# First column tiles of z instead of u, z stored from ScalarE's queue, gated-unit stream buffers lower, squares of x added on VectorE

## Chip, cores and metric

One NeuronCore of a Trainium2 chip runs the whole kernel. The metric is device time in microseconds; the kernel before takes 1092.7 us (median of 3 runs, 1092.6 to 1092.8).

## What is computed

A two-layer decoder trunk over 1024 positions of width 1024, in float32. The change touches layer 0:

```python
xn = rmsnorm(h, g)
u, z = jnp.split(xn @ in_w, [1024], axis=-1)
y = gelu(s5_ssm(u, ...) + d_skip * u)       # diagonal state space model over positions
y = y * sigmoid(y @ glu_w + glu_b)          # gated unit
y = y * silu(z)
h = h + y @ out_w
```

Then follow a shared K/V projection, a layer of differential attention, an out-projection and a last norm. Each float32 product of a matrix is made of three TensorE matmuls of `fp32r` parts.

## The kernel before, in words

Activations lie transposed: 8 row tiles of 128 channels by 1024 positions. `mm3` (L157 to L161) makes one product: high part by high part (L159), low part of the activation (L160), low part of the weight (L161). A column tile of a dense layer is 8 k-steps by 2 halves of 512 positions by these 3 matmuls, 48 in all (`mm_tile`, `dense`). A weight tile is loaded into `mraw` (one buffer), cast to `mhi` on ScalarE (ACT, L749) and its rest `mlo` is made on VectorE (DVE, L750); `mhi` and `mlo` have two buffers each. Accumulators of the dense layers are `ps` (4 banks, so two column tiles) and for the state space model `ps2` and `pb`.

Layer 0 begins while x is still arriving. For each of 8 row tiles of x, ACT casts `xh` and squares the tile (`rt`), DVE makes the rest `xl`, and TensorE (PE) does that k-step for three column tiles of u at once, with weights `fh` and `fl` (`first_u`). The sum of the squares over channels is taken on PE too: 32-column matmuls against ones (L526), in four column tiles of the array. From it come `rcol`, the broadcast row `R` (L688, L537), and the evacuation of u multiplied by `R` (L491). z needs no `R` here: it is evacuated as it is (L494) and multiplied by `R1` (the same row) in the gated unit (L623).

The state space model follows, for 8 channel tiles b, in units `t` (input powers and transposes, L310, L332), `c` (output powers `ca` and Toeplitz blocks, L362, L374 to L384), `u` (a column tile of u, stored to `ud`), `a` (apply: L392 on PE, then a chain of DVE operations from L401 to the last, L415, which writes the states `v`) and `o` (output: L424 on PE against `ca` and `toep`, GELU on ACT, L437, one half of the tile after the other, and a store to `yd` from ACT's queue, L439). `ORDER` lists the units. After them come the tiles 8 to 15 of the in-projection, which are z, and then the gated unit: `load_y` reads each `yd` back into `yr` (L595, issued by SyncE, SP), ACT casts `yh` (L610), DVE makes `yl` (L611), and 8 column tiles against `glu_w` follow. Per tile the gated unit's `done` loads z and y (`z`, `ya`), multiplies both on GpSimd (POOL, L623, L624), takes two sigmoids on ACT (L625 of z, L628 of the accumulator) and multiplies on DVE.

`ORDER` and the written sequence are only the start: the program is built with a scheduler that orders each engine's instructions by a timeline of its own, and every engine then runs its list strictly in order. Buffers with one name are used in turn: `yr` shares the names `ya`, `sg` and `z` (two buffers each) with the gated unit's own tiles.

Of the kernel before, what the change touches and what calls it, by code (L numbers as in the profile page):

```python
# [8 lines left out]
F32 = mybir.dt.float32  # L9
# [9 lines left out]
P = 128  # L19
SEQ = 1024  # L20
D = 1024
KT = D // P
# [11 lines left out]
NEG = -1e30  # L34


ORDER = ("t0 c0 t1 u3 a0 c1 o0 t2 u4 a1 c2 o1 t3 u5 a2 c3 o2 t4 u6 a3 c4 o3 t5 u7 a4 c5 o4 t6 a5 c6 o5 t7 a6 c7 o6 a7 "
         "o7").split()


# [14 lines left out]
class Trunk:  # L55
# [389 lines left out]
    def layer0(self, dbg=None):  # L445
        tc, nc, I = self.tc, self.nc, self.I
# [12 lines left out]
        with ExitStack() as es:  # L459
            sp, ev = pool(es, "ssm", 1), pool(es, "ev", 2)  # L460
            stp = ExitStack()
            tp = pool(stp, "stp", 1)
            R = self.R1
            pcr = self.ps3.tile([P, 2, 512], F32, name="pb")
            sqs = []

            pick = tp.tile([P, 2], F32, name="pick")
            G.memset(pick, 0.0)
            for r in range(4):
                G.memset(pick[32 * r:32 * r + 1, r // 2:r // 2 + 1], 1.0)  # L470

            ga = tp.tile([P, KT], F32, name="ga")
            nc.sync.dma_start(ga, I["ga"])

            def prep_x(k, cuts):
                raw = tp.tile([P, SEQ], F32, name="xraw", bufs=3)
                g = ga[:, k:k + 1]
                for c in cuts:
                    nc.sync.dma_start(raw[:, c], I["xT"][k * P:(k + 1) * P, c])
                    S.activation(xh[k][:, c], raw[:, c], AF.Copy, scale=g)  # L480
                    V.scalar_tensor_tensor(xl[k][:, c], raw[:, c], g, rd(xh[k][:, c]), op0=ALU.mult,
                                           op1=ALU.subtract)
                sqs.append(tp.tile([P, SEQ], F32, name="rt0", bufs=3))
                S.activation(sqs[k], raw, AF.Square)

            def evac(m, pt):
                for h in range(2):
                    hs = slice(h * 512, h * 512 + 512)
                    o = ev.tile([P, 512], F32, name="evo")
                    if m < KT:  # L490
                        V.tensor_mul(o, pt[h], R[:, hs])  # L491
                        nc.sync.dma_start(udv[m][:, hs], o)
                    else:
                        S.copy(o, pt[h])  # L494
                        nc.sync.dma_start(zds[m - KT][:, hs], o)


            pt0 = [[(ps if m < 2 else self.ps2).tile([P, 512], F32, name="ps") for h in range(2)] for m in range(3)]
            fst = ExitStack()
            fp = pool(fst, "first", 1)  # L500
            fw = []
            for k in range(KT):
                raw = fp.tile([P, 3 * P], F32, name="fw", bufs=3)
                hi = fp.tile([P, 3 * P], F32R, name=f"fh{k}")
                lo = fp.tile([P, 3 * P], F32R, name=f"fl{k}")
                nc.sync.dma_start(raw, I["in_w"][k * P:(k + 1) * P, 0:3 * P])
                S.copy(hi, raw)
                V.tensor_sub(lo, raw, rd(hi))
                prep_x(k, (slice(0, 512), slice(512, SEQ)) if k == 0 else (slice(0, SEQ),))
                if k == 0:  # L510
                    self.load_consts()
                    for i, pl in enumerate((tp, sp)):
                        self.load_small(i, pl.tile([P, CUTS[i + 1] - CUTS[i]], F32, name=f"small{i}"))
                fw.append((hi, lo))
            def first_u(k):
                for m in range(3):
                    ms = slice(m * P, (m + 1) * P)
                    self.mm_tile((fw[k][0][:, ms], fw[k][1][:, ms]), pt0[m], xh, xl, k)

            late = KT - 2  # L520
            for k in range(KT):
                if k < late:
                    first_u(k)
                for h in range(2):
                    r = 64 * h + k % 2 * 32
                    nc.tensor.matmul(pcr[r:r + 32, 0, :], self.ones.broadcast_to([P, 32]),  # L526
                                     sqs[k][:, h * 512:h * 512 + 512], start=k < 2, stop=k >= KT - 2,
                                     tile_position=(0, r))
            part = tp.tile([P, SEQ], F32, name="rt0", bufs=3)[:, 0:512]
            S.copy(part, pcr[:, 0, :])  # L530
            for q in range(KT):
                nc.tensor.matmul(pcr[:, 1, q:q + 1], part[:, q % 4 * P:(q % 4 + 1) * P], pick[:, q // 4:q // 4 + 1],
                                 start=True, stop=True)
            S.activation(self.rcol, pcr[:, 1, 0:KT], AF.Identity, bias=self.small1[:, 5:6], scale=1.0 / D)
            G.tensor_tensor(self.rcol, self.rcol, self.mhalf.broadcast_to([P, KT]), op=ALU.pow)
            self.norm_rows([pcr[:, q // 4, q % 4 * P:(q % 4 + 1) * P] for q in range(KT)], self.rcol)
            S.copy(R, pcr.rearrange("p h c -> p (h c)"))  # L537
            for k in range(late, KT):
                first_u(k)
            fst.close()  # L540
            for m in range(3):
                evac(m, pt0[m])
            self.ssm_setup(sp, tp)
            V.memset(self.small1[:, 2:3], SUBLN_EPS)
            V.tensor_scalar(self.small1[:, 0:1], self.sm("subln"), 1.0 - LAM_INIT, None, op0=ALU.mult)
            V.tensor_scalar(self.gq, self.sm("gb"), 0.125, None, op0=ALU.mult)
            stp.close()
            yst = ExitStack()
            yq = yst.enter_context(tc.tile_pool(name="yq", bufs=YQ, side="right", reuse_waits="tile"))
            sb, tb = pool(es, "ssb", 2), pool(es, "sst", 1)  # L550
            self.ks = tb.tile([P, T, P], F32, name="ks")
            G.memset(self.ks, 0.0)
            psb = self.ps3
            t = {}
            ops = {
                "t": lambda b: t.update({b: self.ssm_in(b, sb, tb, self.ps2)}),
                "c": lambda b: self.ssm_tables(b, t[b], sb, tb, self.ps2, dr),
                "u": lambda b: self.dense(I["in_w"], (b,), xh, xl, ps, evac),
                "a": lambda b: self.ssm_apply(b, t[b], sb, tb, psb, uds[b]),
                "o": lambda b: self.ssm_out(b, t[b], tb, self.ps2, yds[b]),  # L560
            }
            for x in ORDER:
                ops[x[0]](int(x[1]))
            self.yraw = []
            for k in range(YQ):
                self.yraw.append(yq.tile([P, SEQ], F32, name="yq"))
                self.load_y(yds, k, self.yraw[k])
            self.dense(I["in_w"], range(8, 16), xh, xl, ps, evac)
        with ExitStack() as es:
            yp, cd, cd1 = pool(es, "y2p", 1), pool(es, "cd", 2), pool(es, "cd1", 1)  # L570
            self.glu(yp, cd, ps, yds, zds)
            yst.close()
            self.out0(cd, cd1, ps)
# [8 lines left out]
            hs = slice(h * 512, h * 512 + 512)  # L582
            self.mm3(pt[h], w[0], w[1], xh[k][:, hs], xl[k][:, hs], k == 0, k == KT - 1)

    def dense(self, src, tiles, xh, xl, ps, done, gain=None):

        for m in tiles:
            wh, wl = self.load_m(src, 0, KT, m * P, P, gain)
            pt = [ps.tile([P, 512], F32, name="ps") for h in range(2)]
            for k in range(KT):  # L590
                self.mm_tile((wh[:, k, :], wl[:, k, :]), pt, xh, xl, k)
            done(m, pt)
# [4 lines left out]
    def glu(self, yp, cd, ps, yds, zds):  # L597
# [19 lines left out]
        def done(m, pt):  # L617
            z = cd.tile([P, SEQ], F32, name="z")
            nc.sync.dma_start(z, zds[m])
            sg = cd.tile([P, SEQ], F32, name="sg")  # L620
            a = cd.tile([P, SEQ], F32, name="ya")
            self.load_y(yds, m, a)
            G.tensor_mul(z, z, self.R1)  # L623
            G.tensor_mul(a, a, z)  # L624
            S.activation(z, z, AF.Sigmoid)  # L625
            for h in range(2):
                hs = slice(h * 512, h * 512 + 512)
                S.activation(sg[:, hs], pt[h], AF.Sigmoid, bias=self.sm("glub")[:, m:m + 1])  # L628
            V.tensor_mul(sg, sg, z)
            V.tensor_mul(sg, sg, a)  # L630
            S.copy(self.y2h[m], sg)
            V.tensor_sub(self.y2l[m], sg, rd(self.y2h[m]))

        self.dense(I["glu_w"], range(8), yh, yl, ps, done)

    def out0(self, cd, cd1, ps):
        nc, I = self.nc, self.I
# [541 lines left out]
```

## Time and profile before

| | us |
|---|---|
| median of 3 runs | 1092.7 |
| the profiled execution | 1093.5 |
| its span, first to last instruction | 1091.7 |
| PE busy | 1061.9 |
| DVE busy | 822.5 |
| ACT busy | 623.9 |
| POOL busy | 235.3 |

The profiled execution is 0.8 us above the median, and 1.8 us of it lie outside the span. PE is busy nearly throughout, so its few gaps, and what it does that need not be done there, are where to look; DVE is close behind in the state space stage.

### The profile page before, as it was taken

The numbers are of one execution on the slowest core, as the hardware profiler recorded it, in microseconds if no ns is written. First come the engines' busy times: TensorE is split into PE (matmuls) and PEld (weight loads), VectorE is DVE, ScalarE is ACT, GpSimd is POOL, SyncE is SP. The second block draws the span as 40 slices with busy tenths as digits, with TensorE's granted clock in tenths as the row PEclk, the third lists the DMA queues.
The fourth block names the chain that finished last, engine by engine and source line by source line (L and its number), as shares of the span: only waits on it lengthen the run. The fifth ranks groups of instructions, "written<-read, shape, count | busy, mean of one in ns | idle before, by whom it ended". The sixth has DMA issues, their size and how long they took to land. (4 is left out here: it accounts for less than half of the span.)

```text
span 1091.7 us, 17715 instructions
## 1 busy us (share of the span) xinstructions
PE 1061.9 (97%) x6308; PEld 908.2 (83%) x6308; DVE 822.5 (75%) x1617; ACT 623.9 (57%) x1396; POOL 235.3 (22%) x237
## 2 busy tenths in 40 slices
PE   7999999999999999999999999999999999899996
PEld 5678888887788888998888898889988898788896
DVE  7789999984577543547898778877698777987475
ACT  6432343332534332436787788767788778785463
POOL 0000000000356112211222122221222222210258
PEclk9999999999899999999999999999999999999998
DMA  8143546544654445313122212222222222553344
GB/s 283 45 136 116 174 151 174 159 151 133 238 193 135 127 140 157 135 42 90 44 85 57 73 56 66 86 56 78 66 53 79 60 84 61 148 175 105 109 134 159
DMA packets 143143, 125.94 MB, mean 115 GB/s; under 512 B 9808, under 2 KB 123216, under 8 KB 143056
## 3 DMA queue, kind: packets, MB, share of 16 engines
q1 hardware_dynamic: 134736, 120.63, 36.0%
q10 hardware_dynamic: 8320, 4.19, 1.3%
q8 instruction: 49, 0.80, 0.3%
q14 instruction: 38, 0.31, 0.1%
HBM read 85.48 MB, written 33.03 MB: 109 GB/s over the span
## 5 line engine op out<-in xcount | busy, mean ns | idle before, releaser
L159 PE MATMUL pm<-h1h,mhi 128*128 128x512 f32 x352 | 139.5, 396 | 1.0 <-DVE xr L767 1.0
L160 PE MATMUL pm<-h1l,mhi 128*128 128x512 f32 x352 | 138.8, 394 | 0.0
L161 PE MATMUL pm<-h1h,mlo 128*128 128x512 f32 x352 | 138.6, 394 | 0.0
L848 ACT ACTIVATE e<-e,tiny 128x256 f32<-128x256 f32 (+7 forms) x128 | 99.3, 777 | 33.6 <-DVE tiny L846 32.5
L846 DVE CUSTOM_DVE_ANT_0 e<-s,tri 128x256 f32<-128x256 f32 (+7 forms) x128 | 94.8, 750 | 11.9 <-PE s L841 6.3
L750 DVE TENSOR_TENSOR mlo<-mraw,mhi 128x1024 fp32r<-128x1024 f32 (+1 forms) x44 | 59.9, 1360 | 42.7 <-ACT mhi L749 42.5
L749 ACT CAST mhi<-mraw 128x1024 fp32r<-128x1024 f32 (+1 forms) x44 | 45.3, 1030 | 76.0 <-PE ps L160 55.0
L159 PE MATMUL ps<-xh,mhi 128*128 128x512 f32 x208 | 82.2, 395 | 1.9 <-DVE evo L491 1.9
L161 PE MATMUL ps<-xh,mlo 128*128 128x512 f32 x208 | 81.9, 394 | 0.0
L160 PE MATMUL ps<-xl,mhi 128*128 128x512 f32 x208 | 81.7, 393 | 0.0
L159 PEld LDWEIGHTS pm<-h1h,mhi 128*128 128x128 f32 x352 | 66.2, 188 | 14.7 <-DVE xr L767 2.4
L161 PEld LDWEIGHTS pm<-h1h,mlo 128*128 128x128 f32 x352 | 66.2, 188 | 12.7
L771 POOL TENSOR_TENSOR xs<-xs,RS 128x512 f32<-128x512 f32 x32 | 42.9, 1340 | 156.0 <-DMA xs<-ze 114.2
L160 PEld LDWEIGHTS pm<-h1l,mhi 128*128 128x128 f32 x352 | 66.2, 188 | 12.2
L840 PE MATMUL s<-k,q 128*128 128x384 f32 (+4 forms) x192 | 67.9, 356 | 3.0 <-DMA q<-z 3.0
L915 POOL TENSOR_TENSOR ob<-ob,sq 128x256 f32<-128x256 f32 x32 | 25.7, 803 | 190.3 <-ACT sq L910 177.9
L841 PE MATMUL s<-k,z 128*128 128x384 f32 (+4 forms) x192 | 65.9, 346 | 0.0
L810 PE MATMUL pm<-mhi,h1h 128*128 128x256 f32 x224 | 64.5, 288 | 1.1 <-DVE z L698 0.8
L735 ACT ACTIVATE mhi<-mraw,small 128x128 fp32r<-128x128 f32 (+1 forms) x152 | 51.8, 414 | 21.5 <-PE ps L160 14.4
L811 PE MATMUL pm<-mlo,h1h 128*128 128x256 f32 x224 | 63.3, 284 | 0.1
L812 PE MATMUL pm<-mhi,h1l 128*128 128x256 f32 x224 | 63.1, 283 | 0.0
L877 DVE TENSOR_TENSOR pl<-t,ph 128x512 fp32r<-128x512 f32 (+2 forms) x112 | 54.9, 492 | 10.8 <-ACT ph L876 10.4
(375 smaller groups left out, 3091.0 us busy)
## 6 DMA issues: line engine op xcount, KB each, us to landing
mraw<-in_kv_w SPq DMA_DIRECT2D x16, 512.0 KB
mraw<-in_b_in_w SPq DMA_DIRECT2D x16, 512.0 KB
mraw<-in_in_w SPq DMA_DIRECT2D x13, 512.0 KB
ud<-evo SPq DMA_DIRECT2D x16, 256.0 KB
ug<-ud SPq DMA_DIRECT2D x8, 512.0 KB
kd<-ks SPq DMA_DIRECT2D x8, 512.0 KB
toep<-kd SPq DMA_DIRECT2D x8, 512.0 KB
yd<-yb ACTq DMA_DIRECT2D x8, 512.0 KB
```

Of the source, the lines that this page charges most:

```text
L159: mm(ps, wh, xh, start=first, stop=False)
L160: mm(ps, wh, xl, start=False, stop=False)
L161: mm(ps, wl, xh, start=False, stop=last)
L750: nc.vector.tensor_sub(lo, raw, rd(hi))
L810: mm(o, self.h1h[k][:, ts], wh, start=k == 0, stop=False)
L811: mm(o, self.h1h[k][:, ts], wl, start=False, stop=False)
L812: mm(o, self.h1l[k][:, ts], wh, start=False, stop=k == KT - 1)
L840: mm(sps[m][:, c, :w], q2[m][:, qt], ks[m][:, cs], start=True, stop=False)
L841: mm(sps[m][:, c, :w], q2[2 + m][:, qt], ks[m][:, cs], start=False, stop=True)
L846: V.tensor_tensor_reduce(out=blocks(em[:, :L]), in0=sp[:, 0:nb, :w], in1=blocks(self.tri[:, SEQ - L:]), scale=-1.0, scalar=3e38, op0=ALU.a ...
L848: S.activation(em[:, :L], em[:, :L], AF.Exp, bias=nmx[:, m:m + 1], scale=-1.0, accum_out=sm[:, m:m + 1])
L877: V.tensor_sub(pl[:, jj, ii, :], tp[:, jj, ii, :], rd(ph[:, jj, ii, :]))
```

## The change

1. The three column tiles that begin while x arrives are now tiles 8 to 10 (z), and `u` tiles 0, 1 and 2 come later: 0 right after the norm, 1 and 2 in `ORDER`. At the end five z tiles are left instead of eight.
2. z is stored by ACT's queue instead of SP's.
3. In the gated unit the pools are opened in another order, so that `yr`, `ya`, `sg` and `z` lie lowest, over what the state space model's tables held, and not over its last work tiles. Its first two column tiles run k-steps 0 to 6 of both before the last k-step of either.
4. The squares of x are added up by 7 DVE additions into `ssum`, and 8 small matmuls (L522 of the changed kernel) sum over channels; the column-tile matmuls, `pick` and `part` are gone.

```diff
-ORDER = ("t0 c0 t1 u3 a0 c1 o0 t2 u4 a1 c2 o1 t3 u5 a2 c3 o2 t4 u6 a3 c4 o3 t5 u7 a4 c5 o4 t6 a5 c6 o5 t7 a6 c7 o6 a7 "
+ORDER = ("t0 c0 u1 t1 u2 a0 c1 o0 t2 u3 a1 c2 o1 t3 u4 a2 c3 o2 t4 u5 a3 c4 o3 t5 u6 a4 c5 o4 t6 u7 a5 c6 o5 t7 a6 c7 o6 a7 "
...
-                sqs.append(tp.tile([P, SEQ], F32, name="rt0", bufs=3))
+                sqs.append(tp.tile([P, SEQ], F32, name="rt0" if k else "ssum", bufs=2 if k else 1))
                 S.activation(sqs[k], raw, AF.Square)
+                if k:
+                    V.tensor_add(sqs[0], sqs[0], sqs[k])
...
                         S.copy(o, pt[h])
-                        nc.sync.dma_start(zds[m - KT][:, hs], o)
+                        nc.scalar.dma_start(zds[m - KT][:, hs], o)
...
-                nc.sync.dma_start(raw, I["in_w"][k * P:(k + 1) * P, 0:3 * P])
+                nc.sync.dma_start(raw, I["in_w"][k * P:(k + 1) * P, D:D + 3 * P])
...
             for k in range(KT):
-                if k < late:
-                    first_u(k)
-                for h in range(2):
-                    r = 64 * h + k % 2 * 32
-                    nc.tensor.matmul(pcr[r:r + 32, 0, :], self.ones.broadcast_to([P, 32]),
-                                     sqs[k][:, h * 512:h * 512 + 512], start=k < 2, stop=k >= KT - 2,
-                                     tile_position=(0, r))
-            part = tp.tile([P, SEQ], F32, name="rt0", bufs=3)[:, 0:512]
-            S.copy(part, pcr[:, 0, :])
+                first_z(k)
+            fst.close()
+            for m in range(3):
+                evac(KT + m, pt0[m])
             for q in range(KT):
-                nc.tensor.matmul(pcr[:, 1, q:q + 1], part[:, q % 4 * P:(q % 4 + 1) * P], pick[:, q // 4:q // 4 + 1],
-                                 start=True, stop=True)
+                nc.tensor.matmul(pcr[:, 1, q:q + 1], sqs[0][:, q * P:(q + 1) * P], self.ones, start=True, stop=True)
...
+            self.dense(I["in_w"], (0,), xh, xl, ps, evac)
...
-            self.dense(I["in_w"], range(8, 16), xh, xl, ps, evac)
+            self.dense(I["in_w"], range(11, 16), xh, xl, ps, evac)
         with ExitStack() as es:
-            yp, cd, cd1 = pool(es, "y2p", 1), pool(es, "cd", 2), pool(es, "cd1", 1)
+            cd, cd1, yp = pool(es, "cd", 2), pool(es, "cd1", 1), pool(es, "y2p", 1)
...
-        for m in tiles:
+        begun = []
+        for m in tiles[:first]:
+            wh, wl = self.load_m(src, 0, KT, m * P, P, gain)
+            begun.append((m, wh, wl, [ps.tile([P, 512], F32, name="ps") for h in range(2)]))
+        for ks in (range(KT - 1), (KT - 1,)):
+            for m, wh, wl, pt in begun:
+                for k in ks:
+                    self.mm_tile((wh[:, k, :], wl[:, k, :]), pt, xh, xl, k)
+        for m, wh, wl, pt in begun:
+            done(m, pt)
+        for m in tiles[first:]:
...
-        self.dense(I["glu_w"], range(8), yh, yl, ps, done)
+        self.dense(I["glu_w"], range(8), yh, yl, ps, done, first=2)
```

Because the scheduler orders the lists anew, the change moves more than its lines say. From the gated unit's third column tile on, the lists are the same as before but for a few rows at the start of layer 1. Three places ahead of that matter.

PE, around the last output unit, `o7` (the last L424). Before, it stands inside the last z tile (`xh_92` and `xh_93` are its k-steps 6 and 7):

```order
L159 MATMUL ps<-xh_92,mhi 128x512
L424 MATMUL ps<-v,ca 128x128 x16
L424 MATMUL ps<-ug,toep 128x128 x8
L160 MATMUL ps<-xl_100,mhi 128x512
L161 MATMUL ps<-xh_92,mlo 128x512
L159 MATMUL ps<-xh_93,mhi 128x512
```

Now all z tiles are done before `a7`, and `o7` stands inside the gated unit's first two column tiles (`yh_2596` is y's k-step 5, `yh_2602` k-step 6):

```order
L161 MATMUL ps<-yh_2596,mlo 128x512
L424 MATMUL ps<-v,ca 128x128 x16
L424 MATMUL ps<-ug,toep 128x128 x8
L159 MATMUL ps<-yh_2602,mhi 128x512
L160 MATMUL ps<-yl_2603,mhi 128x512
L161 MATMUL ps<-yh_2602,mlo 128x512
```

Of the 96 matmuls of those two tiles, 72 now stand before `o7` and 24 (k-steps 6 and 7) behind it; 62 of the 72 stand between the last L392 of `a7` and `o7`.

ACT, around the GELU of channel tile 7 (`yb`, stored to `yd_117`). Before, its two halves stand together, and the first table load for sigmoids comes after the last cast of y:

```order
L610 CAST yh0_2583<-yq_2072 128x1024
L437 ACTIVATE yb_2042<-ps_2043 128x4x128
L437 ACTIVATE yb_2042<-ps_2044 128x4x128
L439 DMA yd_117<-yb_2042 128x8x128
L494 COPY evo_2564<-ps_2514 128x512
L749 CAST mhi_2717<-mraw_2719 128x1024
```

Now the sigmoids of the first two z tiles (`z_2742`, `z_2756`) stand before its first half and between its halves, each with table loads:

```order
L606 CAST yh6_2602<-yr_2600 128x1024
L621 ACT_TABLE_LOAD
L621 ACTIVATE z_2742<-z_2742 128x1024
L437 ACT_TABLE_LOAD
L437 ACTIVATE yb_2211<-ps_2212 128x4x128
L621 ACT_TABLE_LOAD
L621 ACTIVATE z_2756<-z_2756 128x1024
L437 ACT_TABLE_LOAD
L437 ACTIVATE yb_2211<-ps_2213 128x4x128
L439 DMA yd_117<-yb_2211 128x8x128
L606 CAST yh7_2608<-yr_2606 128x1024
```

Between the halves there are now two table loads and one sigmoid of 1024 positions.

SP, the loads of the gated unit. Before, all of y is loaded after the last z tile is stored (`zd_125`):

```order
L495 DMA zd_125<-evo_2567 128x512
L595 DMA yr_2587<-yd_111 128x1024
L595 DMA yr_2593<-yd_112 128x1024
L595 DMA yr_2599<-yd_113 128x1024
L595 DMA yr_2605<-yd_114 128x1024
L595 DMA yr_2611<-yd_115 128x1024
L595 DMA yr_2617<-yd_116 128x1024
L187 DMA glub_2645<-in_small 128x8
```

Now five of them stand ahead of these rows, right behind `c7`'s DVE work, and the loads for the gated unit's first two `done` steps stand ahead of the load of y's last tile (`yr_2606`):

```order
L615 DMA z_2742<-zd_118 128x1024
L384 DMA toep_2145<-kd_2143 128x8x128
L615 DMA z_2756<-zd_119 128x1024
L591 DMA yr_2600<-yd_116 128x1024
L591 DMA ya_2745<-yd_110 128x1024
L591 DMA ya_2759<-yd_111 128x1024
L591 DMA yr_2606<-yd_117 128x1024
```

`ya_2759` takes the buffer of `yr_2600` (y's tile 6), and POOL multiplies it by `z_2756` before ACT may take the sigmoid of `z_2756` in place.

## Rows read from the trace of the kernel before

**Rows 1.** The page, busy time: us, share of the span, instructions

```profile
PE 1061.9 (97%) x6308; PEld 908.2 (83%) x6308; DVE 822.5 (75%) x1617; ACT 623.9 (57%) x1396; POOL 235.3 (22%) x237
```

**Rows 2.** Waits of PE, first 300 us: line, waited for, total, times, longest

```profile
PE ps L159 <- ACT yh L610: 4.3, 1, 4.3
PE ps L159 <- DVE evo L491: 1.9, 1, 1.9
```

**Rows 3.** Busy by stretch: PE, PEld, DVE, ACT, POOL, granted clock, DMA share, GB/s

```profile
42.50:55.74 13.24, 11.33 (x66) 9.66 (x65) 6.77 (x18) 6.88 (x14) 1.66 (x1) 1.00 0.00 0
55.74:247.80 192.06, 191.38 (x1464) 157.93 (x1464) 179.80 (x196) 64.00 (x158) 5.49 (x24) 1.00 0.49 151
...
271.40:275.65 4.25, 0.00 (x0) 0.00 (x1) 0.02 (x1) 1.04 (x1) 0.00 (x0) 0.75 0.93 322
275.65:280.10 4.45, 4.45 (x11) 3.48 (x12) 4.34 (x4) 3.61 (x4) 0.00 (x0) 0.50 1.01 408
```

**Rows 4.** Groups of PE instructions, first 60 us: busy us, mean ns

```profile
L526 PE MATMUL pb<-rt,small 128*32 128x512 f32 x32 | 7.4, 604 | 0.0
```

**Rows 5.** Timeline of PE, 240 to 271 us: start, us, what, idle before

```profile
247.82 0.50 PE L159 MATMUL ps<-xh,mhi 128*128 128x512 f32 x1
...
262.28 0.39 PE L159 MATMUL ps<-xh,mhi 128*128 128x512 f32 x1
262.59 2.06 PE L424 MATMUL ps<-v,ca 64*128 64x128 f32 x32
...
266.39 0.47 PE L160 MATMUL ps<-xl,mhi 128*128 128x512 f32 x1
```

**Rows 6.** Timeline of DVE, first 110 us

```profile
46.22 1.22 DVE L272 TENSOR_TENSOR big<-bm,fi 128x1024 f32<-128x1024 f32 x1
...
54.99 1.29 DVE L491 TENSOR_TENSOR evo<-ps,R 128x512 f32<-128x512 f32 x2 [6.23 <-ACT R L537]
```

**Rows 7.** Timeline of DVE, 238 to 261 us: the chain of a7

```profile
247.93 1.22 DVE L401 TENSOR_TENSOR w<-pb,E 128x1024 f32<-128x1024 f32 x1 [6.07 <-PE pb L392]
...
257.89 0.68 DVE L415 TENSOR_TENSOR v<-w,w 128x508 f32<-128x508 f32 x1
258.49 1.21 DVE L611 TENSOR_TENSOR yl<-yq,yh 128x1024 fp32r<-128x1024 f32 x1
```

**Rows 8.** Timeline of ACT, 265 to 305 us: last GELU's store, casts of y, first sigmoid

```profile
267.30 0.37 ACTq L439 DMA_DIRECT2D yd<-yb  x1
...
274.55 1.04 ACT L610 CAST yh<-yr 128x1024 fp32r<-128x1024 f32 x1 [4.71 <-DMA yr<-yd]
...
284.18 1.05 ACT L610 CAST yh<-yr 128x1024 fp32r<-128x1024 f32 x1 [2.07 <-DMA yr<-yd]
...
291.25 1.06 ACT L625 ACTIVATE z<-z 128x1024 f32<-128x1024 f32 x1 [4.72 <-POOL ya L624]
```

**Rows 9.** Timeline of ACT, 118 to 125 us: the table load for GELU

```profile
120.82 0.61 ACT L350 COPY M<-m 128x508 f32<-128x508 f32 x1 [5.28 <-DVE vs L407]
121.45 1.28 ACT L437 ACT_TABLE_LOAD   x1
122.75 1.09 ACT L437 ACTIVATE yb<-ps 128x512 f32<-128x512 f32 x2
```

**Rows 10.** Timeline of SP's queue, 225 to 305 us: start, time of the issue alone

```profile
227.25 0.32 SPq L382 DMA_DIRECT2D kd<-ks  x1
229.98 0.37 SPq L384 DMA_DIRECT2D toep<-kd  x1
...
243.69 0.32 SPq L382 DMA_DIRECT2D kd<-ks  x1
247.96 0.37 SPq L384 DMA_DIRECT2D toep<-kd  x1
...
270.28 3.12 SPq L595 DMA_DIRECT2D yr<-yd  x6
```

**Rows 11.** Timeline of POOL, 265 to 305 us

```profile
293.68 2.40 POOL L624 TENSOR_TENSOR ya<-ya,z 128x1024 f32<-128x1024 f32 x1
```

More of the change, by code (lines that the diff above doesn't have):

```diff
@@ L465, in layer0 @@
             sqs = []
[L467 to L470, printed above, removed]
             ga = tp.tile([P, KT], F32, name="ga")
@@ L514, in layer0, with first_z @@
                 fw.append((hi, lo))
-            def first_u(k):
+            def first_z(k):
                 for m in range(3):
@@ L518, in first_u @@
                     self.mm_tile((fw[k][0][:, ms], fw[k][1][:, ms]), pt0[m], xh, xl, k)
-            late = KT - 2
             for k in range(KT):
-                if k < late:
-                    first_u(k)
-                for h in range(2):
-                    r = 64 * h + k % 2 * 32
-                    nc.tensor.matmul(pcr[r:r + 32, 0, :], self.ones.broadcast_to([P, 32]),
-                                     sqs[k][:, h * 512:h * 512 + 512], start=k < 2, stop=k >= KT - 2,
-                                     tile_position=(0, r))
-            part = tp.tile([P, SEQ], F32, name="rt0", bufs=3)[:, 0:512]
-            S.copy(part, pcr[:, 0, :])
+                first_z(k)
+            fst.close()
+            for m in range(3):
+                evac(KT + m, pt0[m])
             for q in range(KT):
-                nc.tensor.matmul(pcr[:, 1, q:q + 1], part[:, q % 4 * P:(q % 4 + 1) * P], pick[:, q // 4:q // 4 + 1],
-                                 start=True, stop=True)
+                nc.tensor.matmul(pcr[:, 1, q:q + 1], sqs[0][:, q * P:(q + 1) * P], self.ones, start=True, stop=True)
             S.activation(self.rcol, pcr[:, 1, 0:KT], AF.Identity, bias=self.small1[:, 5:6], scale=1.0 / D)
@@ L537, in layer0 @@
             S.copy(R, pcr.rearrange("p h c -> p (h c)"))
[L538 to L542, printed above, removed]
+            self.dense(I["in_w"], (0,), xh, xl, ps, evac)
             self.ssm_setup(sp, tp)
@@ L583, in mm_tile, with dense @@
             self.mm3(pt[h], w[0], w[1], xh[k][:, hs], xl[k][:, hs], k == 0, k == KT - 1)
-    def dense(self, src, tiles, xh, xl, ps, done, gain=None):
-        for m in tiles:
+    def dense(self, src, tiles, xh, xl, ps, done, gain=None, first=0):
+        begun = []
[9 more added lines that the diff above has]
+        for m in tiles[first:]:
             wh, wl = self.load_m(src, 0, KT, m * P, P, gain)
```

## Prediction

> **What bounds the kernel now.** Begin with the busy shares: PE works 1061.9 us of a span of 1091.7 [rows 1], so 30 us of gaps and whatever PE does needlessly are all that can be won. Then read whom PE waits for in the first 300 us, the only part that the change reorders: 1.9 us for the evacuation of the first u tile behind the norm, and 4.3 us for y before the gated unit [rows 2] (the wait for the first x is not touched). Then the busy table by stretch [rows 3]: in the state space stage, 55.7 to 247.8 us, PE has 191.4 of 192.1 us and DVE 179.8, so PE sets the pace and DVE is 94% behind it. The last two stretches show the gap before the gated unit and what follows it: 4.25 us without a matmul, then 11 matmuls in 4.45 us at a granted clock of 0.50, that is 1.2 GHz. Last, the timelines of PE, DVE, ACT and SP around `a7`, `o7` and y tell who is late for whom at the end of the stage.
>
> **What is removed.** The 32 column-tile records of L526 keep PE 7.4 us [rows 4], in a stretch where it never stops; they go. The 1.9 us wait goes too: z is evacuated without `R`, and when the first u tile needs `R`, its own 48 matmuls have covered the norm. The price of a matmul: 64 of them stand between 247.82 and the end of the one at 262.28 [rows 5], 0.23 us each, so that cover is 11 us. What is late next in its place is nothing on PE. Sum so far -9.3 us.
>
> **What DVE gets.** Seven additions of 128x1024, a new row; the nearest is L272, the same kind and size, 1.22 us [rows 6]: 8.5 us, nothing below that, and at most as much again if they delay the `xl` casts. DVE stood idle 6.2 us just behind this stretch, waiting for `R` at the head of its list [rows 6], and 6.1 us before `a7` [rows 7]. So I take them as hidden, but the cover is nearly used up: that is a rival. The moved column tiles cost PE and DVE the same wherever they stand. The z stores: sixteen issues of 0.37 us on ACT (the row of `yd` [rows 8]) beside 64 us of work in 192 [rows 3]: nothing.
>
> **What moves at the end.** By the lists, z no longer fills PE up to `o7`; the gated unit's k-steps 0 to 5 do. Up to the end of `o7` PE has 80 more matmuls to do than before (8 of z, 72 of y), 18.4 us, less the 9.3 saved: `o7` ends not at 266.4 [rows 5] but near 275.5. Behind it stand k-step 6, 12 matmuls or 2.8 us, and then k-step 7, which needs y's tile 7, which comes out of `o7`. Before, 8 z matmuls and 96 of y stood behind `o7`. So the question is how long the last tile of y takes. In the new lists it is not only GELU, store and load. From the end of `a7`'s last DVE row: `yl` of tile 6, 1.21 [rows 7]; then its buffer is free for the load of `ya`; POOL's product, 2.40 [rows 11]; the sigmoid of the second z, 1.06 [rows 8]; a table load to the next activation, 1.30, and half of a GELU pair, 0.55 [rows 9]; the store of `yd`; the load of `yr`; the cast, 1.05 [rows 8]. The three transfers of 512 KB: a store that SP's next issue waited for took 2.73 us in a quiet queue and 4.27 in a busy one, and the first of six loads 4.27 from issue to cast [rows 10, 8]. Bounds 2.73 and 4.27, I take 3.3, nearer the quiet one since little else moves then. Sum 1.21 + 2.40 + 1.06 + 1.30 + 0.55 + 1.05 + 3 x 3.3 = 17.5 us (15.8 to 20.4). PE has in that time `o7`, 3.8 us, and k-step 6, 2.8, so it idles 10.9 us, if it reaches `o7` when DVE ends. It reaches it 62 matmuls or 14.2 us after the last L392 of `a7`. DVE needs 10.6 us from there [rows 7], less one weight split that moved away, plus the splits of y's tiles 4 and 5, in all 11.7; and y's tiles 1 to 3, loaded only behind `c7`, are split before `a7` begins, which I put 3 us behind that L392. So DVE ends 0.5 us after PE arrives: the new gap is 11.4 us. If y's tiles come early, DVE is 2.5 us ahead and the gap is 8.4; that is the low bound with the middle price of the transfers.
>
> **The rest.** The low clock after the gap stays: 11 matmuls took 4.45 us where 2.5 would do [rows 3, 5], before and after, no term. New is that both weight buffers are held to the end of the first two tiles, so the third tile's cast of 1.05 and split of 1.21 begin only then; four matmuls of the second tile cover part. 1.5 us, between 0 and 3.
>
> **Sum.** -7.4 - 1.9 - 4.25 (old gap) + 11.4 + 1.5 = -0.65 us. The profiled execution of 1093.5 becomes 1092.9; it stands 0.8 above the median, so the run becomes 1092.1, no change that can be told (a measurement here tells 0.2%, 2.2 us).
>
> **A rule against the change.** The row of the GELU load shows that it starts as the copy before it ends (120.82 + 0.61) and that the next activation follows 1.30 us after its start [rows 9]: a switch costs 1.3 us. The Trainium skill (ScalarE: Activation LUTs, What ACT_TABLE_LOAD costs) gives each switch to another set 1.28 us of load and 1.38 of drain, 2.66 in all. By that the one switch on my chain would add 1.4 us and the sum would be +0.7. The row shows no drain, so the sum goes by the row.
>
> **Rivals.**
> *The late tile is no later than the old one.* If the z and y loads land early, so that POOL and the sigmoids are done before `o7` ends, or DVE runs ahead, only GELU, a store, a load and a cast remain behind `o7`: 0.55 + 2 x 3.3 + 1.05 = 8.2 less k-step 6, a gap of 5.4. Sum -6.6: 1086.1. For it: the loads of y now start some 20 us earlier relative to their use. Against it: the lists put `ya`'s load behind `yl` of tile 6, which is behind `a7`. 22%.
> *DVE sets the pace.* Its 94% [rows 3] become more: 8.5 us of additions, and four splits of y before `a7`, 4.9. Its idle 6.2 and 6.1 are gone then. Place: the chain of `a7`; from the point where its first row starts more than 3.5 us behind the last L392, each further us is one on the total, as `o7` then waits. With 5 us more: +4.3, 1097.0, slower. For it: DVE starts its setup for the model late, because the additions push it back. Against it: PE reaches that stage later too, with two u tiles ahead of the first transposes. 18%.
> *x comes too late for a faster PE.* Without L526 a k-step takes 4.2 us instead of 5.1; if x, not PE, then sets the pace, the 7.4 us turn into waits in part, say half: +3.0, 1095.7. So the change would not do what it says. For it: x's loads share the first 25 us with all the tables. Against it: before, PE did not wait for x after the first tile. 10%.
>
> **Numbers.** The forecast, 50%: -3.5 to +2.3 by the bounds of the gap and the weights' wait. Faster by over 0.2%: 0.10 of it and the first rival, 0.32. Slower: 0.04 of it, most of the second and third rival, 0.26. The same 0.42. The range 1086.5 to 1097.0 leaves out the far ends of the first and second rival; the forecast's own is 1089.2 to 1095.0.
>
> **What would show it.** Right: no L526, no wait before the first u tile, PE's first phase ends 7 us earlier; the last L424 ends near 275; then a gap of 8 to 14 us on PE that ends with a cast of y on ACT, a granted clock near 0.50 behind it, and the third gated tile beginning near 296, as before. Wrong: a PE gap under 6 us there (first rival); PE waits for DVE rows L411 to L415 or `ca` inside the state space stage (second); PE waits for `xh` or `xl` before 42 us (third). Anything that moves the layers behind is not foreseen at all.

## The result: 8.3 us slower

The changed kernel takes 1101.0 us (median of 3 runs, 1100.3 to 1101.5) against 1092.7; the ratio is 1.0076, 95% interval 1.0056 to 1.0096. Its profiled execution is the one of 1101.0 us, with a span of 1099.2. That is 7.5 us above the profiled execution before, which is what is explained below.

### The profile page after: what moved, and what is told of

Read it like the earlier page. It is cut to its first block, busy times and chain, and to the rows that moved or that the text cites. A ratio compares the mean times of both kernels' runs of the same rounds, so it can differ in the third digit from the quotient of the medians.

```text
span 1099.2 us, 17641 instructions
## 1 busy us (share of the span) xinstructions
PE 1054.9 (96%) x6276; PEld 909.5 (83%) x6276; DVE 843.6 (77%) x1624; ACT 629.0 (57%) x1399; POOL 238.0 (22%) x232
## 5 line engine op out<-in xcount | busy, mean ns | idle before, releaser
L746 DVE TENSOR_TENSOR mlo<-mraw,mhi 128x1024 fp32r<-128x1024 f32 (+1 forms) x44 | 62.3, 1417 | 23.5 <-ACT mhi L745 23.4
```

Source lines behind the costliest of these rows:

```text
L746: nc.vector.tensor_sub(lo, raw, rd(hi))
```

## The profile after

Line numbers belong to the kernel that was profiled: the cast of y is L610 in the kernel before and L606 in the changed one, its split L611 and L607. The page's busy row, to be held against [rows 1]:

```profile
PE 1054.9 (96%) x6276; PEld 909.5 (83%) x6276; DVE 843.6 (77%) x1624; ACT 629.0 (57%) x1399; POOL 238.0 (22%) x232
```

PE works 7.0 us less, and the kernel is longer all the same. Waits of PE in the first 300 us (who waits, for what; total us, times, longest), against [rows 2]:

```profile
PE ps L159 <- ACT yh L606: 8.8, 1, 8.8
PE ps L424 <- DVE v L415: 7.7, 1, 7.7
PE ps L159 <- ACT xh L474: 6.8, 1, 6.8
PE ps L362 <- DVE ca L311: 2.7, 2, 2.2
PE ps L160 <- DVE yl L607: 0.4, 1, 0.4
```

The wait for the first u tile is gone. Where one gap of 4.3 us stood before the gated unit, there are now two, and PE waits for DVE inside the state space stage (`ca`), which it hardly did before. The same in the busy table by stretch (columns as in [rows 3]):

```profile
55.00:257.74 202.74, 200.04 (x1503) 166.00 (x1501) 188.02 (x205) 69.89 (x164) 5.46 (x24) 0.99 0.48 150
272.85:280.56 7.71, 0.00 (x0) 0.03 (x1) 7.67 (x5) 3.56 (x4) 6.41 (x2) 0.71 0.18 73
280.56:287.07 6.51, 6.51 (x49) 6.29 (x49) 0.99 (x1) 1.77 (x3) 2.21 (x1) 0.55 0.23 81
...
290.07:298.89 8.82, 0.00 (x0) 0.00 (x1) 0.02 (x1) 2.27 (x4) 0.00 (x0) 0.68 0.39 119
298.89:303.32 4.43, 4.43 (x10) 3.47 (x11) 1.21 (x1) 2.71 (x3) 0.00 (x0) 0.50 0.00 0
```

In the first gap (272.85) DVE is busy for 7.67 of 7.71 us, in the second (290.07) nobody is: there a transfer is awaited. Behind each gap PE runs at a lower granted clock, 0.55 and 0.50, so `o7` (49 records) takes 6.51 us.

The timeline of DVE from the end of `c7` to the end of `a7`, against [rows 7]:

```profile
247.51 1.23 DVE L311 TENSOR_TENSOR ca<-w,w 128x1024 f32<-128x1024 f32 x1
248.66 1.22 DVE L746 TENSOR_TENSOR mlo<-mraw,mhi 128x1024 fp32r<-128x1024 f32 x1
250.45 0.23 DVE L375 SCALAR_TENSOR_TENSOR kb<-delta,small,ps 128x16 f32<-128x16 f32 x1 [0.57 <-ACT kb L374]
257.53 1.23 DVE L607 TENSOR_TENSOR yl<-yr,yh 128x1024 fp32r<-128x1024 f32 x1 [6.85 <-ACT yh L606]
259.83 2.52 DVE L607 TENSOR_TENSOR yl<-yr,yh 128x1024 fp32r<-128x1024 f32 x2 [1.08 <-ACT yh L606]
262.27 1.22 DVE L401 TENSOR_TENSOR w<-pb,E 128x1024 f32<-128x1024 f32 x1
...
268.01 4.54 DVE L407 TENSOR_TENSOR_SCAN vs<-M,v 128x512 f32<-128x512 f32 x2
272.58 1.22 DVE L412 TENSOR_TENSOR w<-vs,E 128x1016 f32<-128x1016 f32 x1
273.72 3.36 DVE L413 TENSOR_TENSOR w<-vs,E 128x1016 f32<-128x1016 f32 x1
277.11 2.71 DVE L414 TENSOR_TENSOR v<-w,w 128x508 f32<-128x508 f32 x1
279.74 0.67 DVE L415 TENSOR_TENSOR v<-w,w 128x508 f32<-128x508 f32 x1
```

and POOL in the same stretch:

```profile
266.88 3.48 POOL L619 TENSOR_TENSOR z<-z,R 128x1024 f32<-128x1024 f32 x1 [25.33 <-DMA z<-zd]
...
272.87 3.14 POOL L619 TENSOR_TENSOR z<-z,R 128x1024 f32<-128x1024 f32 x1
275.96 3.31 POOL L620 TENSOR_TENSOR ya<-ya,z 128x1024 f32<-128x1024 f32 x1
```

Three things are to be seen. DVE is late: `a6` begins at 235.39 us, 8.75 later than before. The last matmul L392 of `a7` ends at 257.74 us on PE, 9.9 later than before. Three splits of y, which wait for loads, stand ahead of `a7`'s first DVE row, so `a7` begins 4.5 us behind that matmul, 14.3 later than before. And `a7` itself takes 18.1 us (262.27 to 280.41), where it took 10.6 before: two splits of y stand in it, and four of its rows are much longer than the same rows elsewhere. The pair L407 takes 4.54 us instead of 2.33, L413 3.36 instead of 1.21, L414 2.71 instead of 0.69, together 6.4 us more, and always while one of POOL's products runs: L413 begins while POOL is at work and ends 1.07 us after POOL's row ends (276.01), which is nearly its own duration.

Last, ACT behind `o7`, against [rows 8, 9]:

```profile
286.39 0.60 ACT L437 ACTIVATE yb<-ps 128x512 f32<-128x512 f32 x1 [4.72 <-PE ps L424]
287.00 1.28 ACT L621 ACT_TABLE_LOAD   x1
288.30 1.06 ACT L621 ACTIVATE z<-z 128x1024 f32<-128x1024 f32 x1
289.38 1.28 ACT L437 ACT_TABLE_LOAD   x1
290.67 0.60 ACT L437 ACTIVATE yb<-ps 128x512 f32<-128x512 f32 x1
291.30 0.38 ACTq L439 DMA_DIRECT2D yd<-yb  x1
297.79 1.04 ACT L606 CAST yh<-yr 128x1024 fp32r<-128x1024 f32 x1 [6.53 <-DMA yr<-yd]
```

Between the halves of GELU 7 stand two table loads and a sigmoid, 3.7 us, as the lists had it. From the start of a table load to the next activation it is 1.30 us again, so the trace agrees with the price the sum was made with, and shows no drain beside it.

## The theories

A: POOL's products slow `a7`'s chain. B: y's loads and splits alone make DVE late. C: with three z tiles done early PE has too little left to do beside `a7`, whatever fills it. D: DVE sets the pace of the state space stage and the seven additions push it back. E: the additions lie in idle time. The times of the kernel before, measured beside the runs, were 1092.8 (first four), 1092.9 (next four) and 1093.2 (last four).

In the diffs `self.in_order` makes the scheduler keep the rows that it is given in that order. The runs with the products held back, the products cut and the store first leave PE's list exactly as in the changed kernel. The edits on the additions do not: with them the scheduler orders PE's list anew, above all around `a7`, so their times are not the price of the edited rows alone.

## Experiments on the end of the stage

**The products held back** (`last_v` is one column of the states that `a7` writes last):

```diff
-            G.tensor_mul(z, z, self.R1)
-            G.tensor_mul(a, a, z)
+            p = [G.tensor_copy(self.small1[:, 6:7], self.last_v)] if m < 2 else []
+            self.in_order(p + [G.tensor_mul(z, z, self.R1), G.tensor_mul(a, a, z)])
```

> The POOL products of the gated unit's first two tiles are held back until the last DVE row of a7 (a one-element copy of the states on POOL stands ahead of them); nothing else of PE's, DVE's and SP's lists moves, and the sigmoids of z fall behind GELU 7. Theory A (POOL's products beside DVE stretch the chain of a7): the chain from the first L401 to the last L415 falls from 18.1 us to about 12.3 (10.0 as in the kernel before, plus two splits of y); o7's wait falls from 7.7 to 1.3 to 2.0; the second gap falls from 8.8 to about 5.6, since the four table loads between the halves of GELU 7 are gone; time 1088 to 1091. Theory B (DVE is late because of y's loads and splits alone): the chain stays at 17 to 18 us, o7's wait at 7, only the second gap shrinks; time 1096 to 1099.

1092.9 us, ratio to before 1.000 (0.9992 to 1.0009): 8.1 below the changed kernel, and 2 above the range given. The timeline of DVE in this run:

```profile
268.33 2.33 DVE L407 TENSOR_TENSOR_SCAN vs<-M,v 128x512 f32<-128x512 f32 x2
270.69 1.22 DVE L412 TENSOR_TENSOR w<-vs,E 128x1016 f32<-128x1016 f32 x1
271.83 1.21 DVE L413 TENSOR_TENSOR w<-vs,E 128x1016 f32<-128x1016 f32 x1
273.07 0.69 DVE L414 TENSOR_TENSOR v<-w,w 128x508 f32<-128x508 f32 x1
```

The rows are back at their lengths, the chain takes 11.8 us (theory A said 12.3), PE waits 0.7 us at `o7`. PE's list and the lateness of `a7` (262.59 us) are those of the changed kernel, so A holds and B falls for the chain's length. But the second gap did not shrink to 5.6; it is 9.2 us. ACT shows why:

```profile
278.58 0.60 ACT L437 ACTIVATE yb<-ps 128x512 f32<-128x512 f32 x1 [0.30 <-PE ps L424]
279.20 1.28 ACT L621 ACT_TABLE_LOAD   x1
282.74 1.06 ACT L621 ACTIVATE z<-z 128x1024 f32<-128x1024 f32 x1 [2.26 <-POOL ya L620]
282.75 0.38 ACTq L439 DMA_DIRECT2D yd<-yb  x1
```

GELU 7 is done at 279.2, yet its store is issued at 282.75: it stands in ACT's list behind a sigmoid that waits for POOL.

**The products cut to 16 columns**, in place:

```diff
-            G.tensor_mul(z, z, self.R1)
-            G.tensor_mul(a, a, z)
+            w = slice(0, 16 if m < 2 else SEQ); G.tensor_mul(z[:, w], z[:, w], self.R1[:, w])
+            G.tensor_mul(a[:, w], a[:, w], z[:, w])
```

> The two POOL products of the gated unit's first two tiles take 16 of 1024 columns (the other columns of z and y are left unmultiplied there), and stand where they stood. Theory A: POOL is nearly free during a7, so its chain takes about 12.3 us as with the products held back, o7 waits 1.3 to 2.0 us; the sigmoids stay ahead of GELU 7 with one table load behind them, so the second gap is about 6; time 1088 to 1092. Theory B: chain 17 to 18 us, time 1096 to 1099.

This edit leaves the other columns unmultiplied. 1094.6 us, ratio 1.0018 (1.0007 to 1.0029). The chain takes 11.8 us, `o7` waits 1.2: A again, with POOL's rows where they were but short. The time is above the range given: GELU 7 now waits in ACT's list until both sigmoids are done (282.69), the second of them behind a load of y, and the second gap is 9.9 us.

**The store first**: as the first run, and the sigmoids of these two tiles stand behind the store.

```diff
+        self.last_store = nc.scalar.dma_start(yd.rearrange("g p c -> p g c"), yb)
...
+            self.in_order(([self.last_store] if m < 2 else []) + [S.activation(z, z, AF.Sigmoid)])
```

> As the run with the products held back, and the two sigmoids of z stand behind the issue of yd's last store on ACT instead of one of them ahead of it; nothing else of the lists moves. Theory A2 (the store of y's last tile stood 3.5 us behind a sigmoid that waited for POOL): the store is issued at about 279.3 instead of 282.8, the second gap falls from 9.2 to 5.7, time 1089 to 1090. Rival: the load of y's last tile waits for something else of SP's queue, no change, 1092 to 1093.

1088.6 us, ratio 0.9968 (0.9950 to 0.9986), 4.3 below the first run; the second gap is 6.3 us. Of the lists only that store moved, ahead of the table load and the sigmoid, so the wait behind the sigmoid is shown as the price of the store's place.

**The stream buffers high again**: the line with `cd, cd1, yp` as before.

```diff
-            cd, cd1, yp = pool(es, "cd", 2), pool(es, "cd1", 1), pool(es, "y2p", 1)
+            yp, cd, cd1 = pool(es, "y2p", 1), pool(es, "cd", 2), pool(es, "cd1", 1)
```

> One line of the change undone: the gated unit's stream buffers stand above y2h again, so y's tiles 1 to 7 and z are loaded behind a7. Theory C (with three tiles of z done early, PE has too little to do beside a7's chain whatever fills it): POOL and the splits of y are out of a7's chain, which takes 10.0 us, but PE reaches o7 some 3 us behind the last L392 and waits 7 to 10 us for the chain, then again 4 to 6 us for y's tile 1; no gap ahead of tile 7 of y; time 1090 to 1096, no better than the kernel before. If only the lower stream buffers did the harm: o7 waits under 2 us and the time is 1083 to 1086.

1102.0 us, 1.0089 (1.0075 to 1.0104): no better than the changed kernel, worse than the range of theory C, whose mechanism is what the waits show. `a7`'s chain is undisturbed (259.38 to 269.0), but `o7` waits 9.2 us for it, y's tile 1 costs 5.5 more, the third tile's weights 2.7. So the low buffers are not the harm by themselves: without them PE stands still beside `a7` with nothing to do.

**`a7`'s matmuls ahead of `c7`** (`ssm_apply` cut in two behind L392; the unit `p7` is its first half), with the products held back, and the same with the store first:

```diff
-... t7 a6 c7 o6 a7 o7
+... t7 a6 p7 c7 o6 a7 o7
```

> Products held back as in the first run of this call, and a7's 16 matmuls L392 issued before the unit c7, so that DVE can begin a7 as soon as c7's products are made. Theory A with the rest of the chain: a7's chain begins near 251 us instead of 262, takes 10 to 12.5 us and ends 5 us or more before PE has done its other work, so o7 waits less than 1 us; o7 and the second gap (about 4 to 6 us) come earlier by 8 to 10; time 1081 to 1087. If DVE and PE are only slid against each other (the splits of y come too late for PE): waits for yl of 5 us or more take the place of the wait of o7, and the time is 1088 to 1092.

1089.8 us, 0.9972 (0.9961 to 0.9984). The chain begins at 254.6, not 251 (it waits for L392 until then), and `o7` does not wait for DVE. But y's tiles now come late: PE waits 1.6 us for `yl` and 2.6 for a cast of `yh`. That is a smaller gain than theory A gave. The time lies in the range of the rival, 1088 to 1092, whose waits for y it shows: 4.2 us together, where the rival had 5 or more.

> a7's matmuls ahead of c7, the POOL products behind a7, the sigmoids behind yd's last store; additions on DVE as in the change. Theory A2: the store of y's last tile is issued 2.5 us earlier than with a7's matmuls first alone; time 1086.5 to 1088.5. Rival: y's last tile is bound by the load of y's tile 6 before it, which came late there (issued at 274.4 us), and nothing changes: 1089 to 1090.5.

1090.0 us, ratio 0.9973 (0.9959 to 0.9986): no gain. The store is issued 2.7 us earlier (280.45 against 283.12), y's last cast comes only 1.0 earlier, and the time is the same; where that last microsecond goes was not followed. The rival's number was right, its reason is not shown.

## Experiments on the additions

**One addition left of seven:**

```diff
-                if k:
+                if k == KT - 1:
                     V.tensor_add(sqs[0], sqs[0], sqs[k])
```

> The changed kernel with one of the seven additions of squares left (tiles 1 to 6 are left out of the norm's sum). The scheduler moves other rows with it. Theory D (DVE sets the pace of the state space stage, and the additions push its start back): the first L401 of a1, a2, a3 come near 115, 138 and 160 us, as in the kernel before, instead of 122, 145 and 168; a7's chain begins 5 to 8 us earlier; time 1093 to 1097. Theory E (the additions lie in idle time of DVE; it is late because its setup waits for the first u tile): the rows come within 2 us of where they are now; time 1099 to 1101.

The kernel leaves out six of the seven additions. 1084.8 us, ratio 0.9922 (0.9892 to 0.9953), 16.2 below the changed kernel and twice what theory D gave. The stage begins as D says: a1 is 8.9 us earlier than in the changed kernel, see the table. But the scheduler moves many rows with this edit, so it is no pure price: between the last L392 and `o7` there now stand 15 matmuls of z and 51 of y. `a7`'s chain is 18.2 us long here too, with splits between its rows, and is done 1.6 us before PE reaches `o7`. PE's only long wait left behind x is 6.3 us for y's last tile.

**The squares back in column tiles on PE**, z still first, buffers still low (`sqs` without `ssum`, the column-tile matmuls, `part` and `pick` as in the kernel before, inside the loop over `first_z`):

```diff
-                if k:
-                    V.tensor_add(sqs[0], sqs[0], sqs[k])
...
+                    nc.tensor.matmul(pcr[r:r + 32, 0, :], self.ones.broadcast_to([P, 32]),
+                                     sqs[k][:, h * 512:h * 512 + 512], start=k < 2, stop=k >= KT - 2,
+                                     tile_position=(0, r))
```

> One part of the change undone: the squares go back into column tiles on PE, z stays first, the gated unit's buffers stay low. Theory D (the additions on DVE are what costs): DVE's a1 to a3 begin near 114, 137 and 160 us again, a7 near 246 to 250; PE's first phase is 8 to 9 us longer, but PE had waited for DVE at the end anyway; time 1088 to 1094, 7 us or more below the changed kernel. If PE's time counted one for one: 1108 to 1110.

1086.6 us (1085.7 to 1088.7), ratio to before 0.9943 (0.9930 to 0.9956). PE has 8.4 us of column tiles again, and the kernel is 14.3 us faster than the changed one. All waits of PE in its first 320 us:

```profile
PE ps L159 <- ACT xh L478: 6.7, 1, 6.7
PE ps L362 <- DVE ca L311: 0.8, 1, 0.8
```

There is no gap before the gated unit at all, and no low clock behind it. The windows over `o7` and over what follows it in this run:

```profile
263.90:267.94 4.04, 4.04 (x50) 3.92 (x50) 2.44 (x3) 1.61 (x3) 0.31 (x1) 1.00 0.92 330
267.94:290.00 22.06, 22.06 (x99) 18.08 (x98) 5.90 (x4) 9.39 (x12) 10.97 (x4) 1.00 0.45 153
```

PE reaches `o7` at 263.90, when `a7`'s chain has been done for 2.6 us, and works without a stop in the 22 us behind it, in which y's last tile is stored, loaded and cast (the cast is at 281.03). DVE is earlier again, as theory D says, but 1086.6 lies below its range of 1088 to 1094, and a second thing has changed: with the new lists 44 matmuls of z and 1 of y stand between the last L392 of `a7` (249.58) and `o7`, where the changed kernel has 62 of y and none of z. This is the cover of theory C, by another way. At a4 and a5 DVE is only 2.6 and 2.7 us earlier than in the changed kernel. How much of the 14.3 us belongs to the additions and how much to z beside `a7` no run separates. When DVE reaches the units, first L401 of each, in us of each profile, and the end of `a7`:

| | a1 | a2 | a3 | a6 | a7 | a7 ends |
|---|---|---|---|---|---|---|
| before | 114.86 | 137.84 | 160.18 | 226.64 | 247.93 | 258.6 |
| changed | 122.13 | 144.99 | 167.78 | 235.39 | 262.27 | 280.4 |
| products held back | 122.60 | 145.47 | 168.27 | 235.89 | 262.59 | 274.4 |
| one addition | 113.21 | 136.20 | 160.44 | 227.49 | 245.39 | 263.6 |
| squares on PE | 115.65 | 139.83 | 164.16 | 230.47 | 249.62 | 261.3 |

**The same with both edits of the end** (products held back, store first):

> As the run before, and the POOL products behind a7 and the sigmoids of z behind yd's last store. Theories A and D together: neither additions nor POOL's products in DVE's way; o7 does not wait for DVE by more than 1 us; time 1085 to 1089, below every version that computes all so far. If PE is now the bound (no gap ahead of o7): the column tiles cost what they save and the time is 1088 to 1091.

1086.3 us, ratio 0.9938 (0.9925 to 0.9951): no difference. POOL's products come behind `a7` by themselves here (267.63), and the store is late behind a sigmoid in the run above too (274.28, GELU 7 done at 270.8), but PE has other work meanwhile. So the 8.1 and 4.3 us of the first experiments hold for an end without cover.

**The additions on POOL:**

```diff
-                    V.tensor_add(sqs[0], sqs[0], sqs[k])
+                    G.tensor_add(sqs[0], sqs[0], sqs[k])
```

> The seven additions on POOL instead of DVE. Theory D: a1 to a3 begin 5 to 8 us earlier, as with the additions left out, less what POOL's additions slow DVE down beside them; time 1093 to 1097. Theory E: 1099 to 1101. If POOL (some 2.4 us each) is late for the norm: a wait of PE ahead of the first u tile of up to 5 us.

1092.8 us, ratio 0.9995 (0.9980 to 1.0010), at the low end of D's range (1093 to 1097), and for another reason. a1 begins at 126.27, later than in the changed kernel: DVE has 8.5 us less to do and comes later still. Its timeline and POOL's in the first 30 us:

```profile
13.72 2.40 DVE L65 SCALAR_TENSOR_TENSOR ea<-ea,ea 128x34 f32<-128x34 f32 x1
...
24.92 2.37 DVE L225 TENSOR_TENSOR ang<-small,ex 128x32 f32<-128x32 f32 x1
27.21 0.18 DVE L226 TENSOR_TENSOR ld<-small,ex 128x32 f32<-128x32 f32 x1
```

```profile
13.51 7.68 POOL L480 TENSOR_TENSOR ssum<-ssum,rt 128x1024 f32<-128x1024 f32 x3 [13.07 <-ACT rt L478]
24.35 2.89 POOL L480 TENSOR_TENSOR ssum<-ssum,rt 128x1024 f32<-128x1024 f32 x1 [3.15 <-ACT rt L478]
```

A DVE row of 34 columns takes 2.40 us beside a POOL addition, one of 32 columns 0.18 without. PE waits 9.6 us for `xl` while x arrives. The kernel is still 8 us faster than the changed one, so the lateness of DVE at a1 does not set the time by itself. Here 32 matmuls of z and 24 of y stand between the last L392 and `o7`, which waits 3.0 us; how the 8 us divide was not taken apart.

**Additions on DVE alone, in the kernel before** (u first, eight z tiles at the end, all else as before):

> The kernel before with one part of the change alone: squares added on DVE instead of the column tiles; u stays first, and all eight z tiles are left for PE beside a7. Theory D: PE's first phase is 7 to 9 us shorter, but a1 to a3 come up to 8 us later on DVE than before unless the additions fit where DVE waited for R; time between 1084 (hidden) and 1093 (not hidden). If the norm gets late (additions end after the last tile of x): a wait of PE of 2 to 6 us ahead of the first evacuation.

1091.4 us, 0.9978 (0.9964 to 0.9993), near the end that stands for "not hidden". DVE is late here too (a1 at 120.92, 6.1 later than before), PE waits 2.6 us for the norm and 1.8 for the first u tile, and the gap before the gated unit is 5.0; with eight z tiles beside `a7`, `o7` waits only 0.5 us. So 8.5 us more on DVE and 7.4 less on PE come out at 1.4 us less in all: with z left beside `a7`, a DVE about as late as in the changed kernel does not make the time longer.

**The z stores on SP's queue again:**

```diff
-                        nc.scalar.dma_start(zds[m - KT][:, hs], o)
+                        nc.sync.dma_start(zds[m - KT][:, hs], o)
```

> One part of the change undone: the z stores are issued on SP's queue again. The issues on ACT lie beside idle time: time 1099 to 1103, no difference from the changed kernel. If they hold up ACT's casts: 1096 to 1099. If on SP they hold up the loads behind them: 1103 or more.

1100.6 us (ratio to before 1.0070, 1.0049 to 1.0091): this part of the change does nothing, as forecast. The order of the k-steps in the gated unit's first two tiles, the rest of part 3, was not undone by itself in any run.

## Why the prediction was wrong

Its own steps, one by one.

- **What is removed: right, and too small.** There is no L526 and no wait ahead of the first u tile. At the end of the norm's matmuls PE had done in the changed kernel, by 51.42 us, all that stood before 55.74 in the old one, and 30 matmuls of u besides (6.95 us): 11.3 us gained, where 9.3 were forecast. A k-step takes 4.08 us, as the third rival supposed, and x kept up: that rival is out.
- **"So I take them as hidden": failed.** The seven additions take 8.5 us, as priced, but they are not covered. The idle 6.2 us was read as a store of time. DVE in the changed kernel, where that idle time stood:

```profile
52.37 0.29 DVE L148 TENSOR_TENSOR PW<-big 128x128 f32<-128x128 f32 x1
55.20 0.69 DVE L487 TENSOR_TENSOR evo<-ps,R 128x512 f32<-128x512 f32 x1 [2.54 <-PE ps L161]
55.80 1.22 DVE L271 TENSOR_TENSOR big<-bm,fr 128x1024 f32<-128x1024 f32 x1
```

The small rows of the setup stand behind the additions and ahead of that idle time; the last of them, L148, comes at 52.37 us instead of 44.75. Of the idle 6.2 us, 2.54 stay idle, now for the first u tile, whose evacuation has moved ahead of the setup's wide rows (L272 at 56.93, 46.22 before [rows 6]). So only a part was filled: a1 to a3 follow 7.2 to 7.6 us later than before, a4 and a5 6.6 and 6.5, a6 8.75, and the lateness is not made up in the whole stage. In the sum it returns as the waits for `ca` and `yl` and as the late start of `a7`. What it costs by itself is open: 14.3 us with the squares on PE, but with z beside `a7` besides, and 8.1 us were won with DVE just as late, by holding back the products.
- **"DVE ends 0.5 us after PE arrives": the step that put the time outside the range.** PE waited 7.7 us at `o7`, not 0.5. It reached `o7` 15.1 us behind the last L392, close to the forecast 14.2. `a7`'s first row came 4.5 us behind it, not 3 (the splits of y, whose loads went out at 250.7), and the chain took 18.1 us, not 11.7. 6.4 of that is POOL: the forecast priced its products as a link behind `a7`, and at nothing for the DVE rows beside them. With the products held back, the same PE list and the same late DVE, the wait is 0.7 us and the time 1092.9, near the forecast 1092.1. The price could have been read in the trace of before. The gated unit's DVE rows there:

```profile
303.07 1.22 DVE L750 TENSOR_TENSOR mlo<-mraw,mhi 128x1024 fp32r<-128x1024 f32 x1
304.33 3.31 DVE L632 TENSOR_TENSOR y2l<-sg,y2h 128x1024 fp32r<-128x1024 f32 x1
```

and POOL's beside them:

```profile
303.38 3.19 POOL L623 TENSOR_TENSOR z<-z,R 128x1024 f32<-128x1024 f32 x1 [7.30 <-DMA z<-zd]
306.65 3.26 POOL L624 TENSOR_TENSOR ya<-ya,z 128x1024 f32<-128x1024 f32 x1
```

A split of 128x1024 takes 3.31 us where it begins behind a product, and 1.22 where it begins first; then the product takes 3.19 instead of 2.40 [rows 11]. The Trainium skill (SBUF — State Buffer, Who interferes with whom) states that a DVE instruction with two inputs in SBUF contends with a GpSimd instruction that reads SBUF, that the pair of ports which they share is an exclusive lock, and that the order of issue decides who blocks. The rows agree: the long L413 ends 1.07 us after POOL's product.
- **The late tile: right.** From the end of `a7` to the first matmul on y's last tile 18.5 us passed, forecast 17.5 (15.8 to 20.4); the gap was 8.8, forecast 8 to 14. Two table loads stand on the way where the sum had one; the first ends at 288.28 us, 1.06 behind POOL's product for the sigmoid (287.22 on POOL). The term of 1.5 us for the third tile's weights does not show: PE has no wait for them.
- **The low clock: missed once.** One stretch behind one gap was forecast as no term. The wait ahead of `o7` brought a second: `o7` took 6.51 us at a granted clock of 0.55, against 4.04 at 1.00 in the run with the squares on PE, 2.5 us.

The sum with what was measured, against before: -11.3 to the norm, -4.25 for the old gap, +2.2 more waiting for `ca`, +0.4 for `yl`, +7.7 ahead of `o7`, +2.5 for its clock, +8.8 for the second gap makes +6.1. At the third gated tile PE is 6.8 us behind (303.84 against 297.00), at the end 7.5; the rest was not followed. The wait ahead of `o7` and its clock make 10.2. All other differences from the forecast make -3.5 together: 2.0 more won ahead of the norm, 2.6 less in the gap for the late tile, no 1.5 for the weights, against 2.6 for `ca` and `yl`. So part of the miss was offset by terms that were wrong the other way.

The second rival, 18%, had the engine, the place, the reason (setup begun late because the additions push it back) and the point from which it decides (3.5 us behind the last L392; it was 4.5). By its own rule that start costs only 1.0 us; it had put 5 us of lateness, for 1097.0, the upper end of the range. The rest of the 7.7 us at `o7` is the length of the chain, POOL's part, which no rival named. Both of its signs came: PE waits for `ca` and for L415. The reason given against it came true as well and did not help: PE's first transposes come at 80.78 us, 74.01 before, but DVE, which has no wait above 1.7 us from there to 250 us, stays late by its own work.

The version with z first, low buffers and the squares on PE, 1086.6 us, is faster than both kernels.

## What to carry to other kernels

Before work is moved from the bound engine to the next busiest, follow one unit of that engine's chain from where the work is put to where the bound engine waits for it: idle time on it counts as cover only if it stands behind the new work and ahead of the row that is waited for, and only the part that is still idle when the lists are ordered anew (of 6.2 us, 2.5 became a wait for another tile). Price a POOL instruction by the DVE rows beside it, not only by its own length. And look at what the bound engine has to do beside the last chain of a stage: with 62 matmuls behind `a7` that ran out together with it, the stores, loads and table switches of the late tile stood in the open, in gaps of 7.7 and 8.8 us; in the run with 44 matmuls of z there, and with DVE earlier besides, there was no gap.

## What the runs showed of the hardware

- POOL and DVE on two-input float32 rows do not run side by side: DVE rows grew from 0.18 to 2.40, from 1.21 to 3.36 and from 0.69 to 2.71 us beside POOL products of 2.4 to 3.5 us, and POOL rows grew from 2.4 to 3.1 or more where DVE had begun first. In the run with one addition left, a POOL product that began during a DVE row took 5.42 us, while the four DVE rows beside it kept their lengths.
- With the seven additions on POOL, which was idle, DVE came to a1 later (126.3 us) than with them on DVE itself (122.1).
- A gap of 7.7 us on PE was followed by 6.51 us at a granted clock of 0.55, one of 8.8 us by 4.43 us at 0.50; in the run without gaps the same stretch shows 1.00.
